# One decoder layer on one core: the convolution tail split into turns, compressed values on 64 rows, output weights and residual rows in another order, and a shared edge tile in the local branch

## The chip, the core and the metric

The kernel runs on one core of a Trainium2 chip, in one launch. The metric is the device time in microseconds (us). Runs of this kernel agree within about 0.2%. A profile is one further execution, recorded by the hardware profiler; its span runs from the first to the last instruction, and the execution's own time is a little longer than its span.

Engines as the profile names them: PE multiplies matrices, PEld loads its stationary operand, DVE, ACT and POOL work on vectors, SP only starts transfers (SPq is its queue). Each engine takes its instructions strictly in the order of its own queue, and an instruction that waits holds up all that stand behind it there.

## What is computed

One pre-norm layer over 1024 rows of width 1024, in float32: an input projection, then two mixers side by side, an output projection with a residual add, a SwiGLU feed-forward part and a last norm.

```python
y = u * jax.nn.sigmoid(v)                        # convolution mixer
y = lax.conv_general_dilated(y, w_dw, ...) + b_dw    # causal, width 31
y = layer_norm(y, ln_g, ln_b); return jax.nn.silu(y)
...
o_c = softmax(q . kc) . vc      # 64 compressed blocks
o_s = softmax(q . gathered top-8 blocks of 64 keys) . vs
mask_w = (dist_w >= 0) & (dist_w < WINDOW)       # local branch, WINDOW = 512
o_w = softmax(q . kw - slope * dist_w, mask_w) . vw
out = g0 * o_c + g1 * o_s + g2 * o_w
...
x = x + concat(conv_out, nsa_out) @ w_out
h = rms_norm(x, ffn_norm); x = x + (silu(h @ w_gate) * (h @ w_up)) @ w_down
```

There are 12 query heads in 4 groups of 3, each head 64 wide.

## The kernel before

Every float32 operand of a matmul is split into a high part (`hi`, written by ACT as a cast) and the rest (`lo`, written by DVE or POOL as a difference), and each product is three matmuls: hi by hi, hi by lo, lo by hi. Rows go in tiles of 128 and in two halves of 512 rows (`hf`).

**Order of the work.** The program is written as generators that are woven together: the main generator yields estimated durations, and a side or fill generator is advanced in between. On top of that a scheduler puts the instructions of each engine in order by its own estimate of when they can run. So a change in one generator moves instructions of others too; what the chip executes is the resulting fixed order of each queue.

**Stages.** (1) First half of the input projection, the compression of keys and values (`compress`, `compress_k`, `compress_v`), the compressed branch's scores (`cmp_stage`), and beside them the convolution of the first half: `conv_taps(0)` on DVE, then `conv_tail(0)`. (2) `attention`: its steps are tuples (half, group, tile `i` of 128 query rows, branch); branch 1 is the local window, branch 0 the selected blocks. The second half of the input projection, then the output projection of the first half (`out_proj`) and its feed-forward part are the fill (`fill_all`). (3) Second half: output projection, feed-forward, last norm.

**Weights.** `load_w` starts a transfer on SP into `w_raw` (two buffers), ACT casts it to `w_hi` (L228), POOL subtracts in quarter pieces to `w_lo` (L232).

**`conv_tail`** (L622). For each of four 128-row tiles of a half: two PE transposes into bank `cl` (L628), mean and variance on DVE (L630, L632), the root on POOL (`crs`, L635), the normalised tile `cn` on DVE (L637); two yields and one of 5.0; then two transposes of `cn` into bank `cm` (L643), scale and offset (`cf`, L646), silu, split, and two transfers to `mix_d` (L652).

**`compress_v`** (L556). Four DVE copies write `ah` and `al` twice side by side into `dup` (L562); 24 matmuls with 128 stationary columns from `dup` (L567) give the compressed values on all 128 rows, rows 64 to 127 repeating rows 0 to 63; one split writes `vcs`.

**`attention`**, local branch, `i` from 4 to 7: five key tiles. `scores` (L804) makes the scores on PE, adds distance and mask on DVE (L839, where masked places get a huge value, and the running minimum is kept), exponentiates 640 columns on ACT (L842), and POOL multiplies them by the gate over the sum (L852). `transposed` (L855) turns each key tile of three heads on PE (`pt`, L858) and splits it into `ph` and `pl`; `product` (L864) multiplies them with the values into bank `o` (L875, L876). A product is issued `LAG` = 2 tiles behind its transposes.

**Output projection of the first half** (`fill_all`, L1545 to L1550): `mix_in` loads four pieces of `mix_d` (L1163: high and low part, columns 128 to 255 and 256 to 511), `x_in` loads the residual rows (L1122, four transfers for each half of the columns), then `out_proj` (L1186 matmuls, L1190 add). The first 128 columns come from `first_mix`, loaded much earlier.

## Time and profile before

| | before |
|---|---|
| three runs | 1448.69, 1451.39, 1451.89 us; median 1451.39 |
| the profiled execution | 1450.36 us, its span 1448.7 us |
| granted PE clock, mean | 0.996 |
| busiest | PE 98%, DVE 70%, ACT 54%, POOL 49% of the span |

"x" counts instructions. PE's records overlap, since matmuls are pipelined: the pace is read from one start to the next, not from the durations. An idle time in brackets is followed by what ended it. A granted clock of 1.00 is full speed.

### The profile page before, as it was taken

To read this page: it belongs to the slowest core of one execution; us is meant where nothing else is said; L and a number is where in the kernel's file an instruction comes from. 1 tells how busy PE (TensorE), PEld (TensorE's weight loads), DVE (VectorE), ACT (ScalarE), POOL (GpSimd) and SP (SyncE) were. 2 spreads that over 40 slices of the span, in tenths; PEclk is the share of its full clock that TensorE was granted. 3 is DMA by queue.
4 is the path that set the end of the run, shared out by engine and by line. 5 is a ranking of instruction groups with operands and counts; after the bars stand their busy time and mean duration, and the time that the engine had idled before them with its cause. 6 is when DMAs were issued, how large, how long until landed. Compare 5 with 4: busy or idle time off the path is not lost.

```text
span 1448.7 us, 23428 instructions
## 1 busy us (share of the span) xinstructions
PE 1416.1 (98%) x7989; PEld 1231.0 (85%) x7989; DVE 1018.4 (70%) x2277; ACT 775.2 (54%) x1608; POOL 703.6 (49%) x981
## 2 busy tenths in 40 slices
PE   8999989998999999999999999999999999999997
PEld 7898878987778888888888888788888999999996
DVE  6487776777787877687784775331477987888884
ACT  6333556777765766766666564222526444444443
POOL 5467774776676655555556556545778000000001
PEclk9999999999999999999999999999999999999999
DMA  7346567675577333344253224823335434333311
GB/s 226 86 133 191 166 200 260 186 204 181 175 272 219 87 105 91 98 125 114 69 142 108 79 67 153 263 73 102 88 109 176 123 89 116 88 90 115 117 59 73
DMA packets 234436, 196.12 MB, mean 135 GB/s; under 512 B 14105, under 2 KB 204413, under 8 KB 234318
## 3 DMA queue, kind: packets, MB, share of 16 engines
q1 hardware_dynamic: 234174, 194.41, 44.6%
q8 instruction: 63, 1.03, 0.3%
q14 instruction: 55, 0.45, 0.1%
q10 hardware_dynamic: 144, 0.23, 0.0%
HBM read 160.85 MB, written 33.55 MB: 134 GB/s over the span
## 4 chain that ended last, share of the span: by engine, by line
PE 77%; DVE 7%; ACT 5%; DMA 5%; POOL 4%; issue 2%; SPq 0%; POOLq 0%; ACTq 0%; DVEq 0%
PE gu L1259 17%; PE dn L1284 17%; PE yy L1415 8%; PE pt L858 4%; PE zz L1415 4%; DMA w_raw<-in_w_in_dram 3%; PE vo L148 3%; PE wo L1210 3%; PE wo L1186 3%; PE o L876 2%; PE o L875 2%; PE s L831 2%; PE aa L1415 2%; PE cv L148 2%; POOL w_lo L232 2%
## 5 line engine op out<-in xcount | busy, mean ns | idle before, releaser
L232 POOL TENSOR_TENSOR w_lo<-w_raw,w_hi 128x256 fp32r<-128x256 f32 (+1 forms) x508 | 406.0, 832 | 183.1 <-ACT w_hi L228 174.9
L1259 PE MATMUL gu<-h,w_hi 128*128 128x512 f32 x768 | 258.1, 399 | 0.0
L228 ACT CAST w_hi<-w_raw 128x1024 fp32r<-128x1024 f32 (+1 forms) x147 | 152.9, 1050 | 177.0 <-DMA w_raw<-in_w_in_dram 56.5
L1284 PE MATMUL dn<-w_hi,aw 128*128 128x512 f32 x690 | 241.7, 396 | 0.6 <-DVE x L1287 0.4
L852 POOL TENSOR_SCALAR pr<-pr,l,gates 128x640 f32<-128x640 f32 (+5 forms) x192 | 150.1, 795 | 126.7 <-DVE l L847 102.7
L238 DVE TENSOR_TENSOR pl<-pt,ph 128x384 fp32r<-128x384 f32 x264 | 142.2, 551 | 48.7 <-ACT ph L238 45.5
L842 ACT ACTIVATE pr<-pr,m 128x640 f32<-128x640 f32 (+5 forms) x192 | 141.3, 737 | 59.8 <-DVE m L839 56.5
L1259 PEld LDWEIGHTS gu<-h,w_hi 128*128 128x128 f32 x768 | 142.6, 188 | 26.7
L238 ACT CAST ph<-pt 128x384 fp32r<-128x384 f32 x264 | 121.4, 476 | 71.0 <-PE pt L858 52.2
L1502 POOL TENSOR_TENSOR rs<-rs,mhalf 128x1 f32<-128x1 f32 x4 | 3.3, 832 | 316.8 <-DVE rs L1501 316.7
L1284 PEld LDWEIGHTS dn<-w_hi,aw 128*128 128x128 f32 x690 | 129.4, 188 | 27.6 <-DVE x L1287 2.1
L1259 PE MATMUL gu<-h,w_lo 128*128 128x512 f32 x384 | 152.2, 396 | 0.0
L1287 DVE TENSOR_TENSOR x<-dn,x 128x512 f32<-128x512 f32 x177 | 118.8, 682 | 35.0 <-PE dn L1284 34.6
L1284 PE MATMUL dn<-w_lo,aw 128*128 128x512 f32 x345 | 136.1, 394 | 0.0
L858 PE MATMUL pt<-ident,pr 128*128 128x128 f32 x792 | 129.1, 273 | 0.8 <-DVE pct L707 0.3
L839 DVE CUSTOM_DVE_ANT_0 pr<-s,base 128x384 f32<-128x384 f32 (+3 forms) x192 | 101.5, 533 | 22.6 <-PE s L833 12.4
L858 PEld LDWEIGHTS pt<-ident,pr 128*128 128x128 f32 x792 | 99.5, 140 | 18.9 <-POOL pr L852 1.1
L1361 ACT CAST w_s<-sum 128x512 fp32r<-128x512 f32 x80 | 49.3, 621 | 114.1 <-PE yy L1415 94.8
L148 PE MATMUL zo<-h,w_hi 128*128 128x512 f32 x320 | 107.2, 401 | 1.5 <-ACT w_hi L228 1.5
L831 PE MATMUL s<-kt,q 128*128 128x384 f32 (+3 forms) x288 | 97.3, 340 | 3.8 <-DVE m L839 2.0
L1415 PEld LDWEIGHTS yy<-term,w_s 128*128 128x128 f32 x720 | 93.4, 188 | 5.3
L876 PE MATMUL o<-pl,vt 128*128 128x384 f32 x264 | 94.5, 358 | 3.0 <-DVE pl L238 3.0
(276 smaller groups left out, 3129.2 us busy)
## 6 DMA issues: line engine op xcount, KB each, us to landing
w_raw<-in_w_gate_up_dram SPq DMA_DIRECT2D x48, 512.0 KB, 3.9
w_raw<-in_w_down_dram SPq DMA_DIRECT2D x43, 512.0 KB, 3.6
w_raw<-in_w_in_dram SPq DMA_DIRECT2D x40, 512.0 KB, 4.4
u_raw<-in_w_gate_up_dram SPq DMA_DIRECT2D x20, 512.0 KB, 4.7
g_raw<-in_w_gate_up_dram SPq DMA_DIRECT2D x19, 512.0 KB, 4.0
qc<-q_d SPq DMA_DIRECT2D x16, 384.0 KB, 5.3
pc_d<-pct SPq DMA_DIRECT2D x16, 384.0 KB, 3.2
pct<-pc_d SPq DMA_DIRECT2D x32, 192.0 KB, 3.4
```

Of the source, the lines that this page charges most:

```text
L148: lastpe[0] = pe.matmul(*args, **kw)
L228: act.copy(hi[:, :n], raw[:, :n])
L232: eng.tensor_sub(lo[:, q], raw[:, q], hi[:, q].bitcast(F32))
L238: pair = act.copy(hi, src), dve.tensor_sub(lo, src, hi.bitcast(F32))
L831: pe.matmul(sv, q2[0], kk_[:, 0, kk], start=True, stop=False)
L842: act.activation(pr[:, :n], pr[:, :n], AF.Exp, bias=m, scale=-1.0, accum_out=l3[:, r:r + 1])
L852: pool.tensor_scalar(x_, x_, l3[:, r2:r2 + 1], gates[:, i, c:c + 1], op0=ALU.mult, op1=ALU.mult)
L858: pe.transpose(pt[:, r * P:(r + 1) * P], prs[st][1 + r][:, kk * P:(kk + 1) * P], ident)
L876: pe.matmul(o[:, :384], v, pl, start=False, stop=last)
L1259: pe.matmul(o, w[:, k, :], h2[si][h][k // 4][:, k % 4, :], start=n == 0, stop=n == 3 * KT - 1)
L1284: pe.matmul(o, aws[si][:, a, k, t * P:(t + 1) * P], b[:, 0, h], start=n == 0, stop=n == 5)
L1415: pe.matmul(o, w[:, k, :], h[:, k, :], start=fresh and n == 0, stop=n == 11, skip_group_check=not fresh)
```

## The change

Five edits.

1. `conv_tail` becomes `normed_in(q4)` (transposes, statistics, normalised tile) and the rest. Tile 0 is normalised ahead; in each turn tile `q4 + 1` is normalised before tile `q4` is transposed back. The normalised tiles `cns` have four places in the buffer that held `y`.
2. `compress_v` multiplies `ah` and `al` directly with 64 stationary columns into rows 0 to 63; the copies into `dup` are gone, and two splits instead of one write `vcs`, each from the same 64 rows.
3. For the local branch at `i` of 4 and more (16 steps of 3 heads): after the scores, DVE takes the minimum of the first and the last key tile into the last; exponential, gate and transposes run over four tiles (512 columns). Where one of the two tiles is masked the other is not. After the transposes and the split, `unfold` on POOL writes two new tiles for the first key tile (`far`, the part above the diagonal) and zeroes that part in `ph` and `pl`: four selects.
4. In the attention loop a product of the queue may be issued before the transposes; the first product of a query tile is found by whether its bank exists.
5. The output weights' loads are asked for before the residual rows; the first four row transfers are ordered behind the last weight transfer, and the other four are issued after the first matmul of `out_proj`.

```diff
     def compress_v(ah, al, w2h, w2l):
         o = bank("vc", "o")
-        dup = pa.tile([P, 2, 2, GROUPS, 2, 64], F32R, tag="xc", name="dup", bufs=2)
-        dh, dl = dup[:, 0], dup[:, 1]
-        for c in range(2):
-            for d, a in ((dh, ah), (dl, al)):
-                dve.tensor_copy(d[:, :, :, c, :], a.bitcast(F32).rearrange("p t (g n) -> p t g n", g=GROUPS))
         for g in range(GROUPS):
             n = 0
             for ht in range(2):
-                for a, b in ((dh, w2h), (dh, w2l), (dl, w2h)):
-                    pe.matmul(o[:, g * HD:(g + 1) * HD], a[:, ht, g, :, :], b[:, ht, 0:HD],
+                for a, b in ((ah, w2h), (ah, w2l), (al, w2h)):
+                    pe.matmul(o[0:64, g * HD:(g + 1) * HD], a[:, ht, g * 64:(g + 1) * 64], b[:, ht, 0:HD],
                               start=n == 0, stop=n == 5)
...
-        split(vcs[:, :, 0, :], vcs[:, :, 1, :], o3)
+        for c in range(2):
+            split(vcs[c * 64:(c + 1) * 64, :, 0, :], vcs[c * 64:(c + 1) * 64, :, 1, :], o3)
...
     def conv_tail(hf):
         accs = conv_accs[hf]
-        for q4 in range(4):
-            t = hf * 4 + q4
+        cns = py.tile([P, 2, 30 + 512], F32, tag="y", name="cns").rearrange("p a b -> p (a b)")
+        cns = [cns[:, q4 * 256:(q4 + 1) * 256] for q4 in range(4)]
+
+        def normed_in(q4):
             b = bank("cl", "t")
...
-            cn = py.tile([P, 256], F32, tag="cn", name="cn", bufs=2)
-            dve.tensor_scalar(cn, b[:, :256], mv[:, 0:1], rs, op0=ALU.subtract, op1=ALU.mult)
-            for _ in range(2):
+            dve.tensor_scalar(cns[q4], b[:, :256], mv[:, 0:1], rs, op0=ALU.subtract, op1=ALU.mult)
+
+        normed_in(0)
+        yield 0.0
+        yield 0.0
+        yield CONV_LAG
+        for q4 in range(4):
+            if q4 < 3:
+                normed_in(q4 + 1)
+                yield 0.0
                 yield 0.0
             yield CONV_LAG
+            t, cn = hf * 4 + q4, cns[q4]
             b = bank("cm", "t")
...
+        def folded(st):
+            return st[3] == 1 and st[2] >= 4
...
-            act.activation(pr[:, :n], pr[:, :n], AF.Exp, bias=m, scale=-1.0, accum_out=l3[:, r:r + 1])
+            c0 = 0
+            if folded(st):
+                c0 = P
+                dve.tensor_tensor(pr[:, n - P:n], pr[:, 0:P], pr[:, n - P:n], op=ALU.min)
+            act.activation(pr[:, c0:n], pr[:, c0:n], AF.Exp, bias=m, scale=-1.0, accum_out=l3[:, r:r + 1])
...
+        def unfold(ph, pl):
+            far = [p.tile([P, REP * P], F32R, tag=tag, name=tag, bufs=bufs["ph"]) for tag in ("ph", "pl")]
+            both_ = [[y.rearrange("p (r q) -> p r q", r=REP) for y in xf] for xf in zip((ph, pl), far)]
+            for x3, f3 in both_:
+                pool.affine_select(f3, x3, pattern=[[0, REP], [-1, P]], compare_op=ALU.is_ge, fill=0.0,
+                                   base=-1, channel_multiplier=1)
+            for x3, f3 in both_:
+                pool.affine_select(x3, x3, pattern=[[0, REP], [1, P]], compare_op=ALU.is_ge, fill=0.0,
+                                   base=0, channel_multiplier=-1)
+            return far
...
-            ts = range(size(steps[n])) if n >= 0 else []
+            ts = range(folded(steps[n]), size(steps[n])) if n >= 0 else []
...
-                    ph, pl = transposed(steps[n], k)
-                    yield 0.33
-                    pend.append((steps[n], k, ph, pl))
                     if len(pend) > LAG:
                         yield product(*pend.pop(0))
+                    ph, pl = transposed(steps[n], ts[k])
+                    yield 0.33
+                    if len(pend) == LAG:
+                        yield product(*pend.pop(0))
+                    if folded(steps[n]) and k == m - 1:
+                        pend.append((steps[n], 0, *unfold(ph, pl)))
+                    pend.append((steps[n], ts[k], ph, pl))
...
         set_in(0, pm)
-        x_in(0, 0)
-        x_in(0, 1)
-        yield from out_proj(feed, 0, "z", mix, 0, ahead)
+        feed.ahead(2)
+        with tc.issue_after(asked[0].ins):
+            x_in(0, 0)
+        for n, d in enumerate(out_proj(feed, 0, "z", mix, 0, ahead)):
+            if n == 0:
+                with tc.issue_after(asked[0].ins):
+                    x_in(0, 1)
+            yield d
```

Three places where the queues' order changes. First PE, in stage 1, where the compression of the values (`h`) ends and the last projection of that stage (`zo`) begins, with a tile of the convolution tail (`cl`, `cm`) and compressed scores (`sc`) between. Before:

```order
L148 MATMUL h_1733<-xl,w_hi 128x264
L148 MATMUL h_1734<-xl,w_hi 128x264
L643 MATMUL cm<-ident,cn 128x128 x2
L628 MATMUL cl<-ident,cacc 128x128 x2
L673 MATMUL sc<-kc,qc 128x128 x6
L148 MATMUL zo<-h_0_0_127,w_hi 128x512
```

Of the change:

```order
L651 MATMUL cm<-ident,cns 128x128 x2
L148 MATMUL h_1733<-xl,w_hi 128x264
L628 MATMUL cl<-ident,cacc 128x128 x2
L148 MATMUL h_1734<-xl,w_hi 128x264
L148 MATMUL h_1733<-xh,w_hi 128x264
L681 MATMUL sc<-kc,qc 128x128 x6
L148 MATMUL h_1734<-xh,w_hi 128x264
L148 MATMUL h_1733<-xh,w_lo 128x264
L148 MATMUL h_1734<-xh,w_lo 128x264
L148 MATMUL h_1733<-xl,w_hi 128x264
L148 MATMUL h_1734<-xl,w_hi 128x264
L148 MATMUL zo<-h_0_0_127,w_hi 128x512
```

The second tile's `cm` in the order before stands just behind the last `h`; in the order of the change the `cm` there is the first tile's, a turn older, and it, `cl` and `sc` stand before the last `h` instead of behind them.

Second SP, in stage 2, where the output projection of the first half begins: the pieces of `mix_d`, the rows `x`, the output weights `w_raw`, and what else the queue holds. Before:

```order
L1163 DMA mix<-mix_d 128x4x128
L894 DMA mix_d<-oh 64x3x128
L1163 DMA mix<-mix_d 128x4x256
L1122 DMA x_5724<-in_x_dram 128x512
L802 DMA pct<-pc_d 128x384
L1122 DMA x_5724<-in_x_dram 128x512 x3
L227 DMA w_raw<-in_w_out_dram 128x2x512
L894 DMA mix_d<-oh 64x3x128
L1163 DMA mix<-mix_d 128x4x128
L708 DMA pc_d<-pct 128x768
L1163 DMA mix<-mix_d 128x4x256
L1122 DMA x_5725<-in_x_dram 128x512 x4
```

Of the change:

```order
L1193 DMA mix<-mix_d 128x4x128
L1193 DMA mix<-mix_d 128x4x256
L1152 DMA x_5722<-in_x_dram 128x512 x2
L229 DMA w_raw<-in_w_out_dram 128x2x512
L920 DMA mix_d<-oh 64x3x128
L813 DMA pct<-pc_d 128x384
L1193 DMA mix<-mix_d 128x4x128
L1193 DMA mix<-mix_d 128x4x256
L1152 DMA x_5723<-in_x_dram 128x512 x2
L1152 DMA x_5722<-in_x_dram 128x512 x2
L1152 DMA x_5723<-in_x_dram 128x512 x2
```

Between the high part's pieces of `mix` and the low part's there are two row transfers instead of four, and the `mix_d` store that stood between the two high pieces, with the `pc_d` store between the low ones, is elsewhere.

Third POOL, in stage 2, at the first step that has a shared edge tile: the gate products of one step after the other (`pr`), the weights' rest (`w_lo`), the attention output's rest (`oh`, here kept in `kc`). Before:

```order
L886 TENSOR_TENSOR oh<-ou,oh 64x384
L852 TENSOR_SCALAR pr<-pr,l_5429,gates 128x640 x3
L232 TENSOR_TENSOR w_lo<-w_raw,w_hi 128x256 x8
L852 TENSOR_SCALAR pr<-pr,l_5572,gates 128x640 x3
L886 TENSOR_TENSOR kc<-ou,kc 64x384
L852 TENSOR_SCALAR pr<-pr,l_5679,gates 128x640 x3
L232 TENSOR_TENSOR w_lo<-w_raw,w_hi 128x256 x8
```

Of the change:

```order
L912 TENSOR_TENSOR oh<-ou,oh 64x384
L867 TENSOR_SCALAR pr<-pr,l_5423,gates 128x512 x3
L234 TENSOR_TENSOR w_lo<-w_raw,w_hi 128x256 x8
L867 TENSOR_SCALAR pr<-pr,l_5569,gates 128x640 x3
L912 TENSOR_TENSOR kc<-ou,kc 64x384
L883 AFFINE_SELECT ph<-ph 128x384
L883 AFFINE_SELECT pl<-pl 128x384
L886 AFFINE_SELECT ph<-ph 128x384
L886 AFFINE_SELECT pl<-pl 128x384
L867 TENSOR_SCALAR pr<-pr,l_5676,gates 128x512 x3
L234 TENSOR_TENSOR w_lo<-w_raw,w_hi 128x256 x8
```

The gate products of a local step cover 512 columns instead of 640, and four selects stand in the queue between those of two steps.

## Rows read from the trace of the kernel before

**Rows 1.** The page, busy time of each engine in us, its share of the span, and instructions.

```profile
PE 1416.1 (98%) x7989; PEld 1231.0 (85%) x7989; DVE 1018.4 (70%) x2277; ACT 775.2 (54%) x1608; POOL 703.6 (49%) x981
```

**Rows 2.** Waits of PE in the whole span, by what ended them: us in total, times, longest.

```profile
PE cm L643 <- DVE cn L637: 4.8, 2, 4.5
...
PE o L876 <- DVE pl L238: 3.0, 3, 1.0
PE wo L1186 <- DMA mix<-mix_d: 2.4, 1, 2.4
```

**Rows 3.** The busy time of each engine in short stretches; the column behind POOL is the granted PE clock, then the DMA share and GB/s.

```profile
192.00:196.00 4.00, 0.00 (x0) 0.00 (x0) 3.42 (x9) 2.47 (x6) 3.87 (x6) 0.72 0.16 56
196.00:200.00 4.00, 3.69 (x14) 3.41 (x15) 3.61 (x17) 2.71 (x14) 2.51 (x5) 0.50 0.98 262
200.00:204.00 4.00, 4.00 (x17) 3.21 (x17) 3.86 (x10) 2.08 (x4) 3.54 (x5) 0.93 0.56 161
309.00:313.00 4.00, 2.90 (x15) 2.08 (x14) 1.69 (x5) 3.92 (x16) 2.81 (x4) 1.00 0.70 246
422.00:424.00 2.00, 2.00 (x7) 1.51 (x7) 1.69 (x4) 1.91 (x5) 2.00 (x3) 0.61 1.07 395
424.00:426.00 2.00, 2.00 (x8) 2.00 (x7) 0.35 (x2) 0.10 (x2) 1.84 (x4) 0.54 1.06 402
```

**Rows 4.** PE in order of time in stage 1 (start us, us, instruction): the end of the value compression, the wait, what follows it at a slower pace, and the same kinds of instructions later at full pace.

```profile
191.44 0.42 PE L148 MATMUL h<-xl,w_hi 128*128 128x264 f32 x2
196.31 0.69 PE L643 MATMUL cm<-ident,cn 128*128 128x128 f32 x2 [4.45 <-DVE cn L637]
...
200.61 0.63 PE L148 MATMUL zo<-h,w_hi 128*128 128x512 f32 x2
201.07 0.39 PE L148 MATMUL zo<-h,w_lo 128*128 128x512 f32 x1
...
208.02 0.38 PE L643 MATMUL cm<-ident,cn 128*128 128x128 f32 x2
...
208.38 0.48 PE L148 MATMUL zo<-h,w_lo 128*128 128x512 f32 x1
...
214.50 0.53 PE L673 MATMUL sc<-kc,qc 128*128 128x128 f32 x3
214.87 0.45 PE L148 MATMUL zo<-h,w_lo 128*128 128x512 f32 x1
```

**Rows 5.** The chain of work that ended last, in the same stretch (start us, us, what).

```profile
184.52 6.38 DMA w_raw<-in_w_in_dram
...
191.96 0.47 ACT pct L706
...
192.45 0.55 DVE pct L707
...
195.71 0.55 DVE cn L637
```

**Rows 6.** ACT in order of time in the same stretch: the cast of the next weights, and the second half of the compressed hidden values.

```profile
191.00 1.05 ACT L228 CAST w_hi<-w_raw 128x1024 fp32r<-128x1024 f32 x1 [6.01 <-DMA w_raw<-in_w_in_dram]
...
205.98 0.39 ACT L238 CAST ah<-af 128x256 fp32r<-128x256 f32 x1
```

**Rows 7.** POOL in order of time there: the rest of those weights in four pieces.

```profile
192.13 2.97 POOL L232 TENSOR_TENSOR w_lo<-w_raw,w_hi 128x256 fp32r<-128x256 f32 x4 [5.34 <-ACT w_hi L228]
```

**Rows 8.** SP's queue in order of time in stage 2, at the start of the output projection of the first half.

```profile
408.15 0.37 SPq L1163 DMA_DIRECT2D mix<-mix_d  x1
...
410.63 0.45 SPq L1122 DMA_DIRECT2D x<-in_x_dram  x1
...
411.61 1.37 SPq L1122 DMA_DIRECT2D x<-in_x_dram  x3
...
414.25 0.80 SPq L1163 DMA_DIRECT2D mix<-mix_d  x1
```

**Rows 9.** PE in order of time there, and later in the same stage three transposes with the two matmuls behind them.

```profile
418.22 0.62 PE L1186 MATMUL wo<-w_hi,mix 128*128 128x512 f32 x2
421.27 0.72 PE L1186 MATMUL wo<-w_hi,mix 128*128 128x512 f32 x2 [2.42 <-DMA mix<-mix_d]
...
426.06 0.40 PE L1186 MATMUL wo<-w_hi,mix 128*128 128x512 f32 x1
...
433.42 0.49 PE L858 MATMUL pt<-ident,pr 128*128 128x128 f32 x3
433.67 0.42 PE L876 MATMUL o<-pl,vt 128*128 128x384 f32 x1
433.93 0.39 PE L831 MATMUL s<-kt,q 128*128 128x512 f32 x1
```

**Rows 10.** POOL, groups by line and shape in the whole span: line, instruction, shapes, count | busy us, mean ns of one | idle time before.

```profile
L852 POOL TENSOR_SCALAR pr<-pr,l,gates 128x640 f32<-128x640 f32 x60 | 53.3, 902 | 48.6 <-DVE l L847 41.4 <-PE dn L1284 4.7 <-PE pt L858 2.6
...
L691 POOL TENSOR_TENSOR cs<-cs,cl 128x384 f32<-128x384 f32 x16 | 13.3, 831 | 31.4 <-DVE cl L690 26.4 <-PE h L148 4.3 <-PE pt L701 0.6
...
L425 POOL TENSOR_SCALAR_AFFINE_SELECT cb<-cb 128x512 f32<-128x512 f32 x1 | 0.7, 663 | 0.1
```

**Rows 11.** DVE, the same view: the additions over 192 columns.

```profile
L677 DVE TENSOR_TENSOR cs<-cs,sc 128x192 f32<-128x192 f32 x32 | 10.6, 348 | 0.3
```

**Rows 12.** POOL in order of time in stage 2: a wait at the head of its queue.

```profile
510.51 3.25 POOL L852 TENSOR_SCALAR pr<-pr,l,gates 128x896 f32<-128x896 f32 x3 [7.54 <-DVE l L847]
```

More of the change, by code (lines that the diff above doesn't have):

```diff
@@ L215, in tile_hymba @@
     pace = []
+    asked = []
     def load_w(parts, a, b, eng=pool):
@@ L226, in load_w @@
         for c, src in parts:
-            sp.dma_start(v[:, :, c:c + src.shape[-1]], src.rearrange("(k p) c -> p k c", p=P))
+            asked[:] = [sp.dma_start(v[:, :, c:c + src.shape[-1]], src.rearrange("(k p) c -> p k c", p=P))]
         act.copy(hi[:, :n], raw[:, :n])
@@ L565, in compress_v @@
             for ht in range(2):
-                for a, b in ((dh, w2h), (dh, w2l), (dl, w2h)):
-                    pe.matmul(o[:, g * HD:(g + 1) * HD], a[:, ht, g, :, :], b[:, ht, 0:HD],
+                for a, b in ((ah, w2h), (ah, w2l), (al, w2h)):
+                    pe.matmul(o[0:64, g * HD:(g + 1) * HD], a[:, ht, g * 64:(g + 1) * 64], b[:, ht, 0:HD],
                               start=n == 0, stop=n == 5)
                     n += 1
-        o3 = o[:, :256].rearrange("p (g d) -> p g d", g=GROUPS)
-        split(vcs[:, :, 0, :], vcs[:, :, 1, :], o3)
+        o3 = o[0:64, :256].rearrange("p (g d) -> p g d", g=GROUPS)
+        for c in range(2):
+            split(vcs[c * 64:(c + 1) * 64, :, 0, :], vcs[c * 64:(c + 1) * 64, :, 1, :], o3)
     tail = py.tile([P, 2, 30], F32, name="tail")
@@ L849, in scores @@
                 for r2 in range(REP):
-                    x_ = prs[st][1 + r2][:, :n]
+                    x_ = prs[st][1 + r2][:, c0:n]
                     c = g * 9 + r2 * 3 + 1 + br
@@ L867, in product @@
             dur = 0.32
-            if br == 1 and kk == 0:
+            if (g, i) not in accs:
                 accs[g, i] = bank("o", "o")
```

## The prediction

> **What bounds the kernel now.** I read the page first. PE is busy for 1416.1 of the 1448.7 us of the span, 98%, and no other engine is above 70% [rows 1]. The kernel is bound by PE, with 1448.7 − 1416.1 = 32.6 us in which PE has nothing. A change can shorten it in three ways only: fewer matmul rows, less PE idle time, or fewer stretches at a lower PE clock. Then I read PE's waits by what ended them. Of the 32.6 us only few have a name and a size: 4.8 us before `cm`, nearly all in one wait of 4.5; 2.4 us in one wait of `wo` for a piece of `mix`; three small ones of `o` [rows 2]. The reader is to see that the edits 1 and 5 stand exactly at the two large ones. Then the clock: after the 4.45 us wait it is 0.50 between 196 and 200 us, and after the 2.42 us wait it is 0.61 and 0.54 between 422 and 426 us [rows 3, 4, 9]. So each gap costs twice, once idle and once as a slow stretch behind it. Last, the chain and the timelines of ACT and POOL say what each gap waits for. The `cm` gap: a transfer of weights, issued at 184.52, lands at 191.00; ACT has its cast at the head of its queue, waits 6.01 us for it, and only then does the cast of `pct` at 191.96, which releases DVE at 192.45; the normalised tile `cn` is ready at the end of 195.71 + 0.55 [rows 5, 6]. POOL's `w_lo` waits for the same cast [rows 7]. The tile's chain is thus held by queues in which a weight stands ahead of it.
>
> The sums below are made against the profiled execution, 1450.36 us; the median of the three runs, 1451.39, is 1.03 above.
>
> **Edit 1, the tail a turn ahead (term A).** Now: 4.45 us idle. Behind it, from 196.31 to the `zo` at 200.61, PE does cm 2, cl 2, sc 6 and zo 5 [rows 4] in 4.30 us (its matmuls are counted from that view: 14 between 196 and 200 [rows 3]). At full pace cm and cl take 208.38 − 208.02 = 0.36; sc 2 × (214.87 − 214.50) = 0.74; zo, at (201.07 − 200.61)/2 = 0.23 each, 1.15; together 2.25. So 2.05 is lost to the clock, and 6.5 us in all can be won.
>
> In the new order the `cm` there is the first tile's, normalised a turn earlier; it, cl and sc stand among the last `h`. What is late next? The first is `zo`, for its weights: cast at 191.00 + 1.05 = 192.05, first quarter of `w_lo` at 192.13 + 2.97/4 = 192.87 [rows 6, 7]. PE is through the last `h` at about 191.68 (two of 264 columns, 0.12 each, from 191.44) plus 1.10 of the cm, cl and sc that now stand before, so 192.8: a wait of 0.1 to 0.3 us, I take 0.2. The second is `vc`, the value compression. Between the first `zo` and the first `vc` that needs the second half of `ah` stand 42 zo, cm, cl, one pt, 6 sc and 3 vc in the new order: 9.7 + 0.36 + 0.25 [rows 9] + 0.74 + 0.3, about 11.3 us, so PE is there at 204.3. That half of `ah` is ready at 205.98 + 0.39 = 206.37 now [rows 6]. If it stays there, vc waits 2.1 us; if it comes forward with the rest, nothing. On ACT it stands, in the new order, behind one more cast of weights, so it won't come forward fully; up to 4 us is possible if that transfer is late. I take 1.3. A = 6.5 − 0.2 − 1.3 = **5.0**, bounds 0 (the whole gap moves to vc or zo) and 6.5.
>
> **Edit 5, rows behind weights (term B).** Now: the low part's `mix` piece is issued at 414.25, behind the high part's at 408.15 and four row transfers (0.45 + 1.37 us of issue) [rows 8], and PE waits to 421.27, so it took 7.0 us to land, at a DMA share above 1 and 395 GB/s [rows 3]. 2.42 us idle [rows 9]; the two stretches at 0.61 and 0.54 lose 2 × 0.39 + 2 × 0.46 = 1.7. Together 4.1. The change leaves two row transfers between the pieces instead of four: issue about 0.9 us earlier, and 2 × 256 KB less ahead of it, 512 KB at 400 GB/s or 1.3 us. Besides, ten more matmuls stand between the first use of the high piece and that of the low one, about 2 us at 0.23. Cover of 2.2 to 4.2 us against 2.42: closed, or nearly. On SP the weights' transfer, which needs a free buffer, and the store of `oh`, which needs POOL's last difference, stand ahead of the low piece in both orders; if one of them waits longer than now, the piece waits behind it, which is the lower bound. The rows are needed only by the addition behind the first group of `wo`. B = **3.7**, bounds 0 and 4.1.
>
> The Trainium skill ("TensorE: Matmul & The Clock Gate", Part 1) says that TensorE falls back to half its clock after an idle window of about 3.4 us. By that rule the 2.42 us gap would leave the clock alone and B would be at most 2.4 and the sum 1441. The rows after this gap show 0.61 and 0.54, so I keep the 1.7 in the term; a gap of 4 − 2.90 = 1.10 us at 309 us kept 1.00 [rows 3].
>
> **Edits 3 and 4, the shared tile (term C).** Gone are 16 steps × 3 transposes. Three transposes take 433.67 − 433.42 = 0.25; the 384-column matmul behind them then needs 0.26 to the next instead of 0.23 × 384/512 = 0.17 [rows 9]. So 0.34 for a triple, 16 × 0.34 = 5.4 us of PE. The products are as many as before. ACT loses 48 × 128 columns of exponential and 16 splits, the gates' products shrink from 902 ns to 902 × 512/640 = 722 [rows 10]: ACT and POOL aren't the bound, so nothing. Added on DVE are 48 minima of 128 columns; the nearest addition, over 192, takes 348 ns [rows 11], so 12 to 17 us over the whole span on an engine at 70%, ahead of the exponential of its own step, which runs ahead of PE by a step: nothing directly.
>
> Added on POOL are four selects of 384 columns a step. Rows at hand: a select of 512 columns 663 ns, × 384/512 = 0.50; an addition of 384 columns 831 ns [rows 10]. So 2.0 to 3.3 us a step, 32 to 53 us in all on an engine busy for 49% [rows 1]. The products of the far part and of the tile itself wait for the split and then for these selects, in POOL's in-order queue. In the new order they stand behind the other tiles' products, 4 to 8 us of PE work behind their transposes. Split plus selects come to 3 to 4.5 us when POOL is free, so mostly covered. Behind a select that waits for its split stand the next step's gate products and pieces of `w_lo`, which PE needs a step later. It isn't covered when POOL stands before something that waits: three gate products take 2.7 us, and one such group waited 7.54 us for DVE's `l` [rows 12]. Between no wait and about 1 us in each step I take the lower part, 0.16 on average, 2.6 in all: the rows of `o` behind a split now are three waits with 3.0 us [rows 2]. C = 5.4 − 2.6 = **2.8**, bounds −10 and 5.4.
>
> A page of the Trainium skill speaks against this step: "GPSIMD Engine Reference", § 1, says that GpSimd and VectorE contend for their SBUF interface when VectorE works with two SBUF inputs, as the new minimum does. By it the selects would be slower than 0.83 us beside such work, and C nearer to its lower bound; no run here shows it.
>
> **Edit 2 and the second half's tail (term D).** 24 matmuls stay 24 with the same moving columns, 64 stationary ones instead of 128; the four copies go, one more split comes. PE's time is 0 within 1 us. The second half's tail had no wait of its own worth a row; its order on SP changes. With the small waits that any new order shifts, I put 0 ± 3.
>
> Sum: 5.0 + 3.7 + 2.8 = 11.5. 1450.36 − 11.5 = 1438.9; with the 1.03 between it and the median, **1440**.
>
> **The rivals.** First: the gaps only move. `vc` waits for `ah` or `zo` for its weights, and the low piece of `mix` is still late because the DMA queues are full there [rows 3]. Then A is 1 to 2, B 0, C 2.8: about 1447. For it: both gaps hang on transfers whose landing the change doesn't bring forward much; against it: the new order puts work, not only other waits, into both.
>
> Second, slower: POOL's selects become PE's wait. In each of the 16 local steps the last products wait for four selects, behind gate products and `w_lo` pieces that stand at POOL's head. At 1.5 us a step that is 24 us, and each wait that comes near 2.4 us also costs a slow stretch. 1451.39 − 8.7 (A and B) − 5.4 + 24 = 1461. It decides when the mean wait of a step is above (8.7 + 5.4)/16 = 0.9 us. For it: 7.54 us at POOL's head [rows 12]; against it: POOL is half idle, and the products stand late.
>
> Third: the transposes' place was hidden anyway, or small waits elsewhere eat the gain: 1449 to 1454. Against it: PE is the bound nearly everywhere, and there a removed matmul counts.
>
> **How the numbers follow.** Forecast 0.57, rival one 0.22, rival two 0.12, rival three 0.09. The forecast's own range is 1434 to 1447 (A from 2.5 to 6.5, C from −1 to 5.4, D ± 3, not all at once). The range for 8 in 10 is 1433 to 1452: it takes in rival one and part of three, and leaves out two. About 0.2%, 3 us, is what a measurement tells from no change, so faster means below 1448.5. Faster: 0.57 + 0.17 of rival one = 0.74. Same: 0.05 + 0.02 + 0.05 = 0.12. Slower: 0.10 of rival two and 0.04 of three = 0.14.
>
> **What would show it.** Right: no wait of PE above 1 us around 190 to 206 us and none of `wo` for `mix`; a clock of 1.00 in both stretches; 48 transposes fewer; waits of `o` for the selects under 4 us in all, with 32 to 53 us of selects on POOL. Wrong in A: a wait at `vc` or the first `zo` of several us, with a low clock behind it. Wrong in B: the wait at `wo` is still there, on the low piece or on weights. Wrong in C: the group of `o` that waits for `ph` or `pl` on POOL stands at the head of PE's waits.

## The result and the profile after

The changed kernel takes 1442.98 us (median of 13 runs, 1439.26 to 1448.36), the kernel before 1451.22 (13 runs, 1447.03 to 1456.42). The ratio is 0.9945, 95% interval 0.9931 to 0.9959: 8.0 us less, between 5.9 and 10.0. The 13 runs of a kernel spread over 0.6%, more than the 0.2% of the three that were known before. The prediction said 1440, 11.4 us less than the median then known; the range 1433 to 1452 holds the time. The profiled execution took 1445.14 us, its span 1443.4. That is 5.3 us below the span of before; one execution of each can't be balanced to the last microsecond, and below, sizes come from timed runs and places from traces.

The page, busy time, share of the span and instructions (before: [rows 1]):

```profile
PE 1410.5 (98%) x7941; PEld 1227.1 (85%) x7941; DVE 1031.4 (71%) x2306; ACT 764.7 (53%) x1593; POOL 736.7 (51%) x1043
```

48 matmuls fewer, 62 POOL instructions and 33 us of POOL more. PE's idle time is 1443.4 − 1410.5 = 32.9 us, as before (32.6). So the gaps have not gone; they have moved. PE's waits, in us, times, longest:

```profile
PE zo L148 <- ACT w_hi L230: 2.4, 2, 1.5
PE vo L148 <- DVE gates L314: 2.1, 1, 2.1
PE o L901 <- POOL ph L883: 1.8, 2, 1.4
PE vc L564 <- ACT ah L240: 1.5, 2, 0.9
```

The 4.8 us of `cm` and the 2.4 of `wo` for `mix` [rows 2] are not in the list. In their place stand `vc` (1.5, predicted 1.3), the selects (`ph`, with two smaller entries further down) and a wait of `vo` that the prediction did not have. The two of `zo` lie in stage 2, near 335 and 349 us; before, two such waits came to 1.5. PE in order of time in stage 1 (start, us, instruction, idle before it):

```profile
192.51 0.50 PE L148 MATMUL zo<-h,w_hi 128*128 128x512 f32 x1 [0.49 <-DVE pct L715]
...
202.46 0.24 PE L564 MATMUL vc<-w2h,ah 128*64 128x64 f32 x1 [0.65 <-ACT ah L240]
...
206.00 0.24 PE L564 MATMUL vc<-w2h,ah 128*64 128x64 f32 x1 [0.86 <-ACT ah L240]
...
227.86 0.36 PE L148 MATMUL vo<-w_hi,h 128*128 128x274 f32 x1 [2.11 <-DVE gates L314]
```

The windows of that stretch (the column behind POOL is the granted clock, then DMA share and GB/s; the first rows answer to [rows 3]):

```profile
192.00:196.00 4.00, 3.51 (x16) 2.87 (x16) 3.87 (x11) 2.73 (x12) 4.00 (x7) 1.00 0.40 121
196.00:200.00 4.00, 4.00 (x21) 3.25 (x20) 3.50 (x13) 2.40 (x7) 3.05 (x5) 1.00 0.80 226
...
220.00:224.00 4.00, 4.00 (x34) 4.00 (x33) 2.36 (x6) 0.48 (x1) 1.08 (x2) 1.00 1.10 350
...
226.00:228.00 2.00, 0.14 (x1) 0.17 (x2) 1.18 (x5) 1.51 (x7) 0.00 (x0) 1.00 1.06 377
228.00:230.00 2.00, 2.00 (x14) 2.00 (x15) 0.36 (x2) 1.47 (x10) 0.06 (x1) 0.81 1.07 359
230.00:232.00 2.00, 2.00 (x11) 2.00 (x10) 0.51 (x2) 0.28 (x1) 1.61 (x2) 0.50 1.00 357
232.00:234.00 2.00, 2.00 (x10) 1.74 (x10) 0.51 (x3) 0.64 (x2) 0.00 (x0) 0.84 0.80 285
```

From 192 to 200 us the clock is 1.00 where it was 0.72 and 0.50. But 30 us later the same pair, a gap and a slow stretch, is there: 2.11 us and 2 × (0.19 + 0.50 + 0.16) = 1.7. Who holds `vo`? Read from ACT, in order of time:

```profile
226.01 0.40 ACT L240 CAST m<-cf 128x256 fp32r<-128x256 f32 x1 [5.14 <-DMA mix_d<-m]
226.44 0.37 ACT L240 CAST vv<-vo 128x256 fp32r<-128x256 f32 x1
```

The tail's last `m` has one buffer and waits 5.14 us for a store, issued at 219.35 into full queues (DMA share 1.10 between 220 and 224 us, 1.06 after). Behind it on ACT stands the cast of `vo`, on DVE the copy of the gates that frees the bank, and on PE the next `vo`. The third tile's cast of `m` now comes at 215.30 instead of 211.45 us, so its stores stand on SP behind the attention's first loads (the first is issued at 219.35 instead of 212.06), and the fourth tile's cast, due at 220.9, needs their place.

### The profile page after: what moved, and what is told of

Its sections match the earlier page's. It is cut to its first block, busy times and chain, and to the rows that moved or that the text cites. A ratio compares the mean times of both kernels' runs of the same rounds, so it can differ in the third digit from the quotient of the medians.

```text
span 1443.4 us, 23397 instructions
## 1 busy us (share of the span) xinstructions
PE 1410.5 (98%) x7941; PEld 1227.1 (85%) x7941; DVE 1031.4 (71%) x2306; ACT 764.7 (53%) x1593; POOL 736.7 (51%) x1043
## 4 chain that ended last, share of the span: by engine, by line
PE 79%; DVE 5%; ACT 5%; DMA 5%; POOL 4%; issue 2%; SPq 0%; POOLq 0%; ACTq 0%; DVEq 0%
PE gu L1289 18%; PE dn L1314 16%; PE yy L1445 8%; PE pt L873 5%; PE zz L1445 4%; DMA w_raw<-in_w_in_dram 3%; PE vo L148 3%; PE wo L1216 3%; PE wo L1240 3%; PE o L902 3%; PE o L901 3%; PE s L842 3%; POOL w_lo L234 2%; PE aa L1445 2%; PE cv L148 2%; PE zo L148 2%
## 5 line engine op out<-in xcount | busy, mean ns | idle before, releaser
L1289 PE MATMUL gu<-h,w_hi 128*128 128x512 f32 x768 | 251.6, 397 | 0.0
L867 POOL TENSOR_SCALAR pr<-pr,l,gates 128x512 f32<-128x512 f32 (+5 forms) x192 | 145.5, 770 | 106.7 <-DVE l L862 84.5
L857 ACT ACTIVATE pr<-pr,m 128x512 f32<-128x512 f32 (+5 forms) x192 | 136.1, 709 | 93.8 <-DVE m L850 50.6
L240 DVE TENSOR_TENSOR pl<-pt,ph 128x384 fp32r<-128x384 f32 x248 | 134.0, 550 | 42.3 <-ACT ph L240 36.3
L240 ACT CAST ph<-pt 128x384 fp32r<-128x384 f32 x248 | 114.3, 474 | 64.2 <-PE pt L873 39.4
L873 PE MATMUL pt<-ident,pr 128*128 128x128 f32 x744 | 124.6, 275 | 3.3 <-DVE m L850 1.5
L873 PEld LDWEIGHTS pt<-ident,pr 128*128 128x128 f32 x744 | 93.9, 141 | 21.4 <-DVE m L850 2.3
L901 PE MATMUL o<-ph,vt 128*128 128x384 f32 x264 | 96.1, 364 | 3.5 <-POOL ph L883 1.8
```

The source lines that it names most:

```text
L240: pair = act.copy(hi, src), dve.tensor_sub(lo, src, hi.bitcast(F32))
L857: act.activation(pr[:, c0:n], pr[:, c0:n], AF.Exp, bias=m, scale=-1.0, accum_out=l3[:, r:r + 1])
L867: pool.tensor_scalar(x_, x_, l3[:, r2:r2 + 1], gates[:, i, c:c + 1], op0=ALU.mult, op1=ALU.mult)
L873: pe.transpose(pt[:, r * P:(r + 1) * P], prs[st][1 + r][:, kk * P:(kk + 1) * P], ident)
L901: pe.matmul(o[:, :384], v, ph, start=False, stop=False)
L1289: pe.matmul(o, w[:, k, :], h2[si][h][k // 4][:, k % 4, :], start=n == 0, stop=n == 3 * KT - 1)
```

## The experiments

Eleven timed runs and one measurement by itself. "us" is the ratio less 1, times the median of the runs of before beside it (1455.58, 1453.08 or 1451.24).

| run | edits in it | ratio, 95% interval | us against before |
|---|---|---|---|
| tail_alone | 1 | 1.0040, 1.0026 to 1.0054 | +5.8 |
| vc_alone | 2 | 1.0033, 1.0020 to 1.0046 | +4.8 |
| rows_alone | 5 | 1.0023, 1.0009 to 1.0036 | +3.3 |
| fold_alone | 3, 4 | 0.9972, 0.9957 to 0.9988 | −4.1 |
| tail_vc | 1, 2 | 0.9947, 0.9927 to 0.9967 | −7.7 |
| no_fold | 1, 2, 5 | 0.9937, 0.9917 to 0.9957 | −9.2 |
| no_fold_again | 1, 2, 5 | 0.9948, 0.9933 to 0.9963 | −7.5 |
| no_rows | 1, 2, 3, 4 | 0.9956, 0.9940 to 0.9973 | −6.4 |
| no_tail | 2, 3, 4, 5 | 0.9995, 0.9980 to 1.0011 | −0.7 |
| full_again | all | 0.9947, 0.9935 to 0.9959 | −7.7 |
| m_places | all, and more places for `m` | 1.0022, 1.0008 to 1.0036 | +3.2 |

The edits alone add up to +5.8 + 4.8 + 3.3 − 4.1 = +9.8 us; together they are −8. So no edit has a price of its own here.

**Edit 1 alone.**

```diff
...
+            if q4 < 3:
+                normed_in(q4 + 1)
...
+            t, cn = hf * 4 + q4, cns[q4]
...
```

> The kernel before with edit 1 alone (the tail's next tile normalised a turn ahead). Theory: the 4.45 us gap before the second cm and the slow stretch behind it go, but the gain is given back about 30 us later, where ACT's cast of the tail's last m waits for an earlier mix_d store to land, DVE's split waits for ACT, the copy of the gates for DVE, and PE's next vo for that copy. Then PE idles 1.5 us or more at vo near 228 us with a clock of about 0.5 behind it, and the time is 0 to 2.5 us below before. Rival: the wait at vo is made by the other edits (the shorter value compression brings vo forward); then edit 1 alone has no wait above 1 us between 190 and 240 us and gains 4 to 6.5 us.

Measured +5.8 us: theory and rival both fell. The gap before `cm` went, but the value compression, which still has its copies, came to stand in PE's way. PE, then the windows:

```profile
205.94 0.44 PE L711 MATMUL pt<-ident,pg 128*128 128x128 f32 x2 [1.17 <-POOL pg L705]
208.04 0.42 PE L567 MATMUL vc<-w2h,dup 128*128 128x64 f32 x1 [1.67 <-DVE dup L562]
```

```profile
208.00:212.00 4.00, 3.96 (x14) 3.48 (x15) 3.94 (x9) 0.94 (x2) 1.54 (x2) 0.50 0.38 98
212.00:216.00 4.00, 4.00 (x18) 3.92 (x19) 3.84 (x9) 2.48 (x6) 2.71 (x4) 0.50 1.10 362
216.00:220.00 4.00, 4.00 (x11) 3.12 (x10) 2.27 (x6) 2.76 (x14) 0.81 (x2) 0.50 0.77 249
```

2.8 us of waits and twelve at half the clock, 6 us lost, are more than the 6.5 us that the old gap cost. That is 2.3 of the 5.8 us. The rest is not shown: the trace has later waits that before has not, 1.6 us near 356 (for a weight) and 1.5 and 1.4 us at `wo` near 426 and 440, but the 2.42 us for `mix` are gone. The first two copies into `dup` took 1.90 us here, against 0.76 in the kernel before, with POOL's `w_lo` beside them. Half of the rival's mechanism holds: PE waits only 0.4 us at `vo` here, and ACT's cast of `m` doesn't wait for a store. That wait, 5.0 to 5.8 us, is in the traces with edits 1 and 2 together (but that of `m_places`) and in no other.

**Edits 1 and 2.** To the kernel of edit 1 alone is added:

```diff
...
-                dve.tensor_copy(d[:, :, :, c, :], a.bitcast(F32).rearrange("p t (g n) -> p t g n", g=GROUPS))
...
+                    pe.matmul(o[0:64, g * HD:(g + 1) * HD], a[:, ht, g * 64:(g + 1) * 64], b[:, ht, 0:HD],
...
```

> The kernel before with edits 1 and 2 (tail ahead, value compression without the copies). In the run of edit 1 alone PE waited 1.17 us for pg and 1.67 us for dup near 206 us, with the clock at 0.50 for some 12 us behind it. Theory: the copies, on a DVE that POOL holds up, are what eats edit 1's gain; without them the waits at vc stay under 2 us, the clock stays at 1.00 there, and the time is 5 us or more below that of edit 1 alone, so between 1 us above and 5 us below before. Rival: the copies are beside the point and some other wait takes their place: at least 3 us above before.

Measured −7.7, by the two ratios 13.5 us below edit 1 alone, more than the theory's range and in its direction. The waits at `vc` are 0.58 and 0.87 us, the clock there is 1.00. As far as the intervals tell, these two edits make the whole gain of the change (0.9947, all five 0.9945).

**Edit 2 alone.**

```diff
-        dup = pa.tile([P, 2, 2, GROUPS, 2, 64], F32R, tag="xc", name="dup", bufs=2)
...
```

> The kernel before with edit 2 alone (value compression without the copies). Edits 1 and 2 together measured 0.9947, edit 1 alone 1.0040. Theory: edit 2 only matters where edit 1 has brought the value compression forward, since before it the copies are covered by the wait before the second cm: within 2 us of before, the wait of about 4 us before that cm still there. Rival: edit 2 gains by itself and edit 1 adds little: 4 us or more below before.

Measured +4.8: both fell. PE's waits (us, times, longest):

```profile
PE cm L639 <- DVE cn L633: 4.3, 2, 4.0
...
PE pt L854 <- POOL pr L848: 1.7, 2, 0.9
...
PE vo L148 <- DVE gates L312: 1.5, 1, 1.5
```

The gap before `cm` is there as the theory says, and waits of `vo` and `pt` come behind it that before did not have. The profiled execution, 1451.64 us, is 4 us below the median of its runs (1455.76), so its trace can't show the whole loss, and the cause stays open.

**Edit 5 alone.**

```diff
+        feed.ahead(2)
+        with tc.issue_after(asked[0].ins):
+            x_in(0, 0)
...
```

> The kernel before with edit 5 alone (output weights asked for before the residual rows). Theory: the 2.42 us gap at the low piece of mix and the slow stretch behind it go and nothing takes their place: 3 to 4.5 us below before. Rival: the gap goes only because the shared edge tile brings other matmuls between the pieces; then 1 us or more of it is still there and the gain is under 1.5 us.

Measured +3.3. The wait for `mix` is gone as the theory has it, but another takes its place right there. PE and DVE there:

```profile
424.97 0.65 PE L872 MATMUL o<-pct,vcs 128*128 128x384 f32 x1 [4.17 <-DVE ou L882]
```

```profile
418.40 3.56 DVE L722 TENSOR_TENSOR ib<-ib,ft 128x32 f32<-128x32 f32 x1
```

And DVE of the kernel before at the same place in the program:

```profile
416.45 3.56 DVE L720 TENSOR_TENSOR ib<-ib,ft 128x32 f32<-128x32 f32 x1
...
421.96 0.55 DVE L880 TENSOR_TENSOR ou<-o,ou 64x384 f32<-64x384 f32 x1
```

An addition of 32 columns, whose median is 0.19 us, takes 3.56 in both. In the kernel before, PE waited for `mix` until 421.27 and then had matmuls of `wo` up to 423.87, its `o`; by then `ou`, late from the same DVE stall, was ready (421.96 + 0.55). In the new order `o` stands ahead of the low piece's matmuls and PE does not wait for `mix`, so PE is there earlier, and `ou` is what it waits for. One gap hid the other. A second one of the kind comes at 507 us, where before had 1.05 us; PE, and DVE ahead of it:

```profile
506.81 0.80 PE L860 MATMUL pt<-ident,pr 128*128 128x128 f32 x3 [3.47 <-DVE m L841]
```

```profile
500.26 6.02 DVE L254 SCALAR_TENSOR_TENSOR rows<-x,rs,rows 128x1024 f32<-128x1024 f32 x1
```

The product of 1024 columns took 1.86 us in before at that place. Behind both waits the clock falls to 0.50.

**Edits 3 and 4 alone.**

```diff
+                dve.tensor_tensor(pr[:, n - P:n], pr[:, 0:P], pr[:, n - P:n], op=ALU.min)
...
+                        pend.append((steps[n], 0, *unfold(ph, pl)))
```

> The kernel before with edits 3 and 4 alone (shared edge tile, order of the products). Theory: 5.4 us of transposes go, waits of o for the selects on POOL of 1.5 to 3.5 us come, other small waits of o for splits go: 2.5 to 5 us below before. Rival: the selects hold up POOL's gate products, and the gain is eaten: within 1.5 us of before.

Measured −4.1: the time is the theory's, the mechanism is not. The trace has no wait of `o` for a select that its list shows (0.2 us and more), and the gain need not all be the tile's. The gap before `cm` is 4.1 us instead of 4.45, that for `mix` 1.7 instead of 2.42, and behind it the clock stays at 1.00, where the kernel before lost 1.7 us [rows 3]:

```profile
424.00:426.00 2.00, 2.00 (x12) 1.82 (x11) 0.53 (x2) 0.33 (x2) 1.92 (x3) 1.00 1.07 400
```

That is up to 2.7 of the 4.1. Against it stand waits of `dn`, 3.4 us instead of 0.4, and one of 1.5 for `m` near 498.

**More places for `m`.** On the changed kernel:

```diff
-            m2 = [py.tile([P, 2, P], F32R, tag=f"m{i}", name="m2") for i in range(2)]
+            m2 = [cn.bitcast(F32R).rearrange("p (c t) -> p c t", c=2), py.tile([P, 2, P], F32R, tag="m1", name="m2", bufs=2)]
```

> The changed kernel, but the high half of the tail's m is written over its own normalised tile (four places) and the low half has two buffers instead of one, so that a cast needn't wait for the store of the tile ahead of it. Theory: the wait of vo near 228 us and the slow stretch behind it (2.11 + 1.7 us in the changed kernel's trace) go: 2.5 to 4.5 us below the changed kernel, 10 to 12.5 us below before. Rival: the transfers that share the queues there are the bound, and the wait comes back at the next thing that they deliver: within 1 us of the changed kernel.

Measured +3.2, 11 us above the changed kernel. The wait of `vo` went, and 7 us later PE waited for `pg`. POOL and PE of this run:

```profile
232.72 0.24 POOL L580 COPY y<-tail 128x60 f32<-128x60 f32 x1 [9.13 <-DMA pct<-pc_d]
...
233.83 0.84 POOL L703 TENSOR_TENSOR pg<-cs,gates 128x384 f32<-128x384 f32 x1
```

```profile
234.72 0.55 PE L709 MATMUL pt<-ident,pg 128*128 128x128 f32 x3 [3.69 <-POOL pg L703]
```

The second half's `y` shares the buffer that now holds `m` until its stores land, so POOL stood 9.13 us. Which transfer it was the row doesn't settle: it names the last one to land. Its mechanism is the rival's, a wait that comes back at the next thing the queues deliver; its size is nobody's. Of the 11 us the trace shows some: the wait of `pg` is 1.6 longer than that of `vo` was, `cv` waits 2.85 us for a weight at 403 us, with the clock at 0.50 behind it, and two of 1.5 for DVE come near 514 and 520. Places for `m` that nothing else waits for were not tried.

**Without edits 3 and 4.**

```diff
-                c0 = P
-                dve.tensor_tensor(pr[:, n - P:n], pr[:, 0:P], pr[:, n - P:n], op=ALU.min)
...
```

> The changed kernel without edits 3 and 4 (edits 1, 2 and 5). Theory: the shared tile is worth the same with the others as alone (4.1 us), so this is 2 to 6 us below before. Rival: edits 1, 2 and 5 gain nothing together and the whole gain comes from the shared tile or from an order that all five make: within 1.5 us of before or above it.

Measured −9.2 (12.1 to 6.2 below): the rival fell, and the theory's 2 to 6 is too small.

**Without edit 5.**

```diff
-        feed.ahead(2)
-        with tc.issue_after(asked[0].ins):
-            x_in(0, 0)
...
+        x_in(0, 0)
+        x_in(0, 1)
```

> The changed kernel without edit 5. Theory by the prediction's term B: the gap at the low piece of mix is back (1 to 2.5 us, a slow stretch if it is over 2), and the time is 2 to 5 us above the changed kernel, 3 to 6 us below before. Rival: edit 5, which alone made the kernel slower, is worth nothing here either: 7 us or more below before.

Measured −6.4 (8.7 to 3.9 below), which doesn't tell theory from rival. The gap at `mix` is 0.95 us, with the clock at 1.00 behind it; in the run of edits 1 and 2 it is 1.21. So edit 5 had at most that to win here, not 4.1.

**Without edit 1.**

```diff
...
-                normed_in(q4 + 1)
...
```

> The changed kernel without edit 1. Theory: edit 1 wins 4.5 us near 193 us and gives 3.8 of it back near 228 us, so without it the gap before the second cm is back and the time is within 1.5 us of the changed kernel, 6.5 to 9.5 us below before. Rival by the prediction's term A: 4 to 6 us above the changed kernel, 2 to 4 us below before.

Measured −0.7: 7.0 us (1451 × (0.9995 − 0.9947)) above the changed kernel. The theory fell. Without edit 1 ACT's cast of `m` doesn't wait for a store, as the theory has it, but at the same place ACT waits for a weight, and PE 1.66 us at `vo` behind it:

```profile
230.28 1.05 ACT L230 CAST w_hi<-w_raw 128x1024 fp32r<-128x1024 f32 x1 [3.80 <-DMA w_raw<-in_w_in_dram]
```

The gap before `cm` is 5.7 us. The rival, term A, is nearer. (The profiled execution, 1458.43 us, is the slowest of its runs, 6 us above their median.)

**The changed kernel again, beside the same without edits 3 and 4.** The second differs from the first as above.

> The changed kernel as it is, beside the same without edits 3 and 4 on the same chip. Theory: the shared tile gains 4.1 us of transposes (48 at 0.085 us from start to start) and gives it back in waits of its own in the second half of the attention, so the two are within 2 us of each other. Rival: the shared tile keeps its gain of 4 us, and this one is 3 us or more faster.

> The changed kernel without edits 3 and 4, once more. Theory: within 2 us of the changed kernel in the same rounds, 7 to 11 us below before. Rival, that the first measurement was of a chip that favoured it: 3 us or more above the changed kernel.

Measured 0.9947 and 0.9948, medians 1443.27 and 1442.17. Both theories held: the tile is worth nothing in this company that intervals of about 2 us would show. From PE's timelines between 440 and 905 us, start to next start without the named idle, a transpose costs 0.085 us in both, so the 48 save 4.1. What takes it back? In the windows of the changed kernel's second run:

```profile
496.00:498.00 2.00, 1.04 (x7) 0.81 (x7) 1.81 (x6) 1.15 (x3) 2.00 (x4) 0.95 0.00 0
498.00:500.00 2.00, 2.00 (x8) 1.70 (x7) 1.18 (x4) 1.51 (x3) 2.00 (x4) 0.50 0.00 0
500.00:502.00 2.00, 2.00 (x14) 2.00 (x13) 1.51 (x4) 0.88 (x2) 1.31 (x3) 0.70 0.44 130
```

The waits behind which this stands are of `o` and `pt` (0.8 us for a select, 0.6 for DVE's `m`); the slow stretch costs 1.7. In the changed kernel's first run the same two waits (0.81 and 0.54) left the clock alone:

```profile
496.00:498.00 2.00, 1.19 (x8) 0.95 (x7) 1.45 (x5) 1.10 (x4) 2.00 (x4) 1.00 0.00 0
498.00:500.00 2.00, 1.88 (x15) 1.36 (x13) 1.93 (x6) 1.71 (x4) 2.00 (x4) 1.00 0.14 40
```

There the waits of `o` for selects are 3.0 us instead of the 1.2 of the second run. And each of the six traces with the tile has three waits of `dn`, 1.9 us in all, near 1006 to 1030 us, which no trace without it has there. DVE and POOL of the changed kernel there:

```profile
1009.95 2.31 DVE L240 TENSOR_TENSOR aw<-af,aw 128x512 fp32r<-128x512 f32 x1 [1.88 <-ACT aw L240]
```

```profile
1009.34 2.38 POOL L252 TENSOR_TENSOR rows<-rows,grow 128x1024 f32<-128x1024 f32 x1
```

DVE's difference, 0.69 us elsewhere, takes 2.31 and ends 0.5 us after POOL's long product. PE waited 1.15 us for it. The tile's later order has put the two beside each other. The two traces without the tile have a wait of 0.9 us near 896 instead, for `o_lo` on POOL. So the first run gives back 3.0 + 1.9 − 0.9 = 4.0 us and the second 1.2 + 1.7 + 1.9 − 0.9 = 3.9, against 4.1 saved. Other small waits differ too, so this is an account and not a proof. The waits of `dn` are there with the tile alone as well; what that run had besides, the shorter gap for `mix` without its slow stretch, edits 1 and 2 bring without the tile (1.21 us, clock 1.00).

**DVE beside POOL, by itself.**

```diff
...
+                for k in range(N):
+                    stream()
...
+                for k in range(N):
+                    one()
...
```

> A kernel that leaves the whole computation out: it copies x to the output, and runs four short kinds of DVE instructions (two inputs of 32 columns; one input of 3 columns; a minimum of two inputs of 128 columns; a copy of 128 columns), twelve of each, first with POOL idle and then beside twelve POOL instructions back to back of each of three kinds (difference of 256 columns, one-input product of 512 columns, select of 384 columns). Theory: DVE and POOL exclude each other on their way to the on-chip memory; beside a POOL instruction that takes it, a DVE instruction of 0.15 to 0.35 us takes until POOL's instruction, or its whole burst, is over: 0.8 us to several us. Rival: the long DVE instructions in the traces come from what they read (a semaphore, a late operand that the record counts as busy time), and all twelve take 0.15 to 0.5 us beside POOL too.

Measured, duration in ns, least, median and longest of twelve: the two-input addition with POOL idle, beside differences, beside one-input products and beside selects; the copy with POOL idle, beside differences and beside selects.

```profile
L94 DVE TENSOR_TENSOR dtt<-da,db x12: 182/192/193, 10.2 to 12.7; 128x32 f32<-128x32 f32 x12
L94 DVE TENSOR_TENSOR dtt<-da,db x12: 181/396/762, 24.0 to 28.7; 128x32 f32<-128x32 f32 x12
L94 DVE TENSOR_TENSOR dtt<-da,db x12: 182/200/647, 64.6 to 68.8; 128x32 f32<-128x32 f32 x12
L94 DVE TENSOR_TENSOR dtt<-da,db x12: 180/554/555, 109.5 to 115.1; 128x32 f32<-128x32 f32 x12
L97 DVE COPY dcp<-da x12: 218/227/228, 20.5 to 23.3; 128x128 f32<-128x128 f32 x12
L97 DVE COPY dcp<-da x12: 217/766/768, 54.5 to 62.0; 128x128 f32<-128x128 f32 x12
L97 DVE COPY dcp<-da x12: 217/553/555, 132.2 to 137.8; 128x128 f32<-128x128 f32 x12
```

The minimum does as the copy (292 alone, 766 beside differences, 554 beside selects); the one-input instruction of 3 columns has the same median, 170, with a longest of 635. Beside one-input products the copy takes 246 and the minimum 324, little more than alone. POOL's difference takes 729 ns, its product 786 and its select 523 on average. The differences stay between 722 and 782 ns, so DVE is the one that waits. Beside differences and selects a DVE instruction with two inputs, or a copy, thus mostly takes as long as one POOL instruction, as if only one of the two could run; beside one-input products it mostly doesn't. The theory holds to that length here, not to a whole burst; the rival fell. The 2.31 us beside a product of 2.38 are of that size. The 3.56 us beside pieces of 0.7 us each are not. POOL of the kernel before, there:

```profile
415.89 2.85 POOL L232 TENSOR_TENSOR w_lo<-w_raw,w_hi 128x256 fp32r<-128x256 f32 x4
418.71 0.83 POOL L695 TENSOR_TENSOR pg<-cs,gates 128x384 f32<-128x384 f32 x1
419.51 0.44 POOL L714 TENSOR_TENSOR im<-cs 128x128 f32<-128x128 f32 x1
```

POOL's unbroken run ends at 419.95 and DVE's addition at 420.01; with edit 5 alone the two ends are 421.91 and 421.96. Three more DVE instructions of the kernel before, over 3 columns and 0.17 us as a rule, took 2.46, 2.32 and 1.65 us and ended within 0.1 us of the end of such a run. That is the theory's whole burst. What decides between one POOL instruction and the run stays open.

## Why the prediction was right, and where not

**Direction and time** came out: 8.0 us less, 11.4 said. The terms did not.

**Edits 1 and 2** (A and D). The reading of the gap was right: it and its slow stretch went, `zo` waited 0.49 us for 0.2 said (for `pct` on DVE, not for its weights), `vc` 1.5 for 1.3 (0.65 of it on the first half of `ah`, which the sum did not have). Two steps failed. One: "the four copies go ... PE's time is 0 within 1 us". The copies stand in the way of edit 1: with them it costs 5.8 us, without them the pair wins 7.7, where A and D had 5.0. Two: the list of what is late next ended at `vc`. It should have gone on until the queues of the next stretch, where the DMA share is above 1 and ACT waits 5.14 us for a store: `vo` waits 2.1 to 2.8 us in all traces with edits 1 and 2 but that of `m_places`, where `pg` takes its place.

**Edit 5** (B). 3.7 said. 3.3 us slower alone; with the others not to be told from nothing to 1.5 (0.9956 without it and 0.9947 with it, 0.9947 for edits 1 and 2 alone, 0.9937 and 0.9948 with it added). The step that failed: "Now: ... Together 4.1". That is the size of the gap in the old order. Edits 1 and 2 had already brought it to 1.2 us with no slow stretch, and the tile alone to 1.7. The step did not look, either, for what the gap was hiding: DVE's 3.56 us in the same place.

**Edits 3 and 4** (C). 2.8 said, 4.1 measured alone, nothing in the full change. Terms: a triple of transposes was taken as 0.34 us and is 3 × 0.085 = 0.26, since the matmul behind it is no slower on average (0.20 us for one of 384 columns with and without). Selects: 0.50 to 0.83 us each said; 36.5 us for 64 are 0.57. Waits of `o` for them: 2.6 us said, 3.0 in the first trace and 1.2 in the second of the changed kernel. The second rival, with its 0.9 us a step, thus fell. What was missing is the price of longer DVE instructions and the waits of `dn`; and since up to 2.7 of the 4.1 us alone are B's gap and its slow stretch, the terms could not be added.

The Trainium skill ("GPSIMD Engine Reference", § 1) says that GpSimd and VectorE contend where VectorE has two SBUF inputs or works in a two-port mode. For two inputs the measurement by itself agrees beside differences and selects (0.19 to 0.40 and 0.55 us), but beside one-input products, which the page does not set apart, it shows hardly anything (0.20). The copy has one input (0.23 to 0.77 beside differences); that it works in such a mode no run shows. I had drawn from the page that the selects would be slower than 0.83 us. They took 0.57.

So the total was near by luck in part: A and D brought 2.7 us more, and B and C some 6 less, than said. The chance of 0.57 was for a sum of which only the first term was there.

## What to carry to other kernels

Where a scheduler places all queues, price edits as a set: here three that win together each lose alone, so one run without each edit says more than a run of each by itself. Before a gap is priced, look at what the other engines do under it, and follow the work that comes forward until it meets full DMA queues. A stream of differences or selects on POOL beside DVE is not free, even if neither is the bound.

## What the runs showed of the hardware

The clock doesn't follow from the length of a gap alone. The two runs of the changed kernel above show it between 496 and 500 us, with 1.00 in one and 0.50 in the other behind the same two waits. Windows of two runs with the same wait of `vo`, 2.10 and 2.08 us, first edits 1 and 2, then edits 1, 2 and 5:

```profile
228.00:230.00 2.00, 1.23 (x10) 1.26 (x11) 0.59 (x3) 1.82 (x11) 0.00 (x0) 1.00 1.05 331
...
242.00:244.00 2.00, 0.98 (x5) 0.73 (x6) 1.41 (x9) 2.00 (x8) 1.04 (x3) 1.00 0.55 163
244.00:246.00 2.00, 2.00 (x9) 1.90 (x9) 1.81 (x8) 1.44 (x6) 2.00 (x6) 0.51 0.64 183
```

```profile
230.00:232.00 2.00, 2.00 (x14) 2.00 (x13) 0.52 (x3) 1.27 (x7) 0.53 (x1) 0.66 1.07 368
232.00:234.00 2.00, 2.00 (x11) 2.00 (x11) 0.35 (x2) 0.00 (x0) 1.14 (x2) 0.50 0.96 271
```

In the first the clock stays, and falls to 0.51 after some short waits near 243 us (the longest 0.88); in the second it falls at once. What else decides, these runs don't show. Where PE waits often, the 1.7 us of a slow stretch behind a gap thus belong in the range, not in the sum.
